# Row sums of relu: the last 16 rows of each partition in five pieces instead of seven

## The chip, the cores and the metric

The kernel runs on one core of one Trainium2 chip. The metric is the device time of one execution in microseconds (us), the median of several runs. A profile of one execution stands beside it: a record of what each engine and each DMA did, with its own span, which is shorter than the device time.

Engines that matter here: ScalarE (ACT in the profile), VectorE (DVE) and SyncE (SP), whose queue issues all the DMAs. TensorE does nothing. The 16 DMA engines move data between the chip's main memory (HBM) and the on-chip memory of 128 partitions (SBUF).

## The reference

```python
x = np.random.randn(32, 512, 1024).astype(np.float32)

def reference(x):
    relu_x = np.maximum(x, 0)
    return np.sum(relu_x, axis=-1).astype(np.float32)
```

There are 32 x 512 = 16384 rows of 1024 fp32 numbers, 67.1 MB. Each row gives one number, the sum of its positive elements. Every element is read once, so the work is a stream from HBM with a little arithmetic behind it.

## The kernel before

The 16384 rows are spread over 128 partitions, 128 rows each (`J`). They are taken in three regions (`REGIONS`): 1, 111 and 16 rows of each partition. Within a region, a partition's rows lie one after another in HBM, so a DMA of n rows has one contiguous run of n x 4096 bytes for each partition.

The first 112 rows of a partition come in seven chunks of 16 rows (`CHUNKS`, DMAs at L91) into three buffers of `buf` (`NB`), used in turn. SP waits on `s_dve` until a buffer has been read before it issues the DMA that overwrites it. Six chunks are worked on by both engines in series: ACT writes relu in place (L145), DVE sums it (L160). From chunk 6 on, each engine does whole rows by itself in one instruction with an accumulated sum: `on_act` (L127) is an activation with `accum_out`, `on_dve` (L130) a tensor_scalar with max and add. Each such instruction is followed by a short read of its accumulator, which appears as a line of its own in the profile.

The last region, 16 rows of each partition, is the tail. It goes into the buffer that chunk 4 had, and all its loads are issued one behind the other by SP when that buffer is free, at about 122 us; they queue behind chunk 6. There are seven pieces:

- 8, 4 and 2 rows (`TAIL`, L101). Each has its own semaphore. When a piece is in, DVE takes its even rows and ACT its odd rows (L184), each sum going straight into its column of `res`.
- The last two rows, 2048 columns of each partition, in four pieces. `first` is columns 0 to 912 (`CUT`), `second` is 1536 to 2048, `third` is 1280 to 1536, all into `buf` (L112). The fourth, columns 912 to 1280, goes into a small tensor `seam` (L115), from its third column on.

These two rows are cut in ways that do not follow the rows, so partial sums are needed. `first` is halved: ACT sums columns 0 to 456 into `seam` column 0, DVE 456 to 912 into `seam` column 1. ACT sums `second` and DVE sums `third` into the two last columns of `seam`. In `seam` the partial sums of the first row then stand to the left of that row's remaining 112 columns, and those of the second row to the right of its remaining 256 columns. One last instruction on each engine sums such a stretch (relu leaves the partial sums, which are not negative, as they are): ACT 2 + 112 = 114 columns for the first row, DVE 256 + 2 = 258 for the second. Both wait until `s_seam` is 16 + 2, which is the seam piece (16) and the two sums of `second` and `third`; ACT waits for `s_half` too, for the halves of `first`.

Results leave in three stores from `res`. The first 128 rows go early (through `turned`, L117). The 111 columns of the middle region are stored at L123 once chunk 6 is summed and the semaphore `s_in[-1]` says that `third` is in, so that the store is not ahead of the last loads. The last 16 columns are stored at L207 after both last instructions (`s_last`). SP then waits for all stores.

The order on each engine is the order in which the program is written. There is no scheduler.

Of the kernel before, what the change touches and what calls it, by code (L numbers as in the profile page):

```python
# [3 lines left out]
P = 128  # L4
D = 1024
BIG = 16
NB = 3
REGIONS = [1, 111, 16]
CHUNKS = [[(0, 0, 1), (1, 0, 15)]] + [[(1, 16 * c + 15, 16)] for c in range(6)]
ACT_STEPS = [[16], [7, 9], [7, 9], [7, 9], [4, 5, 7], [3, 4, 5]]  # L10
DVE_STEPS = [[4, 5, 7], [7, 4, 5], [7, 4, 5], [7, 4, 5], [4, 5, 7], [3, 4, 5]]
TAIL = [8, 4, 2]
CUT = 912
HEAD = 256


def bass_relu_sum_kernel(
# [14 lines left out]
    fp32 = mybir.dt.float32  # L32
# [4 lines left out]
    B, S, _ = x.shape  # L37
    J = B * S // P
    NBIG = len(CHUNKS)
    assert BIG * NBIG + sum(TAIL) + 2 == J == sum(REGIONS)  # L40

    xr = x.rearrange("b s d -> (b s) d")
    of = out.rearrange("b s -> (b s)")
# [1 line left out]
    xv = [  # L45
        xr[P * s : P * (s + n), :].rearrange("(p j) d -> p j d", p=P)
        for s, n in zip(start, REGIONS)
    ]
    ov = [of[P * s : P * (s + n)].rearrange("(p j) -> p j", p=P) for s, n in zip(start, REGIONS)]

    buf = nc.alloc_sbuf_tensor("buf", [P, NB, BIG, D], fp32)
    w = D - CUT
    seam = nc.alloc_sbuf_tensor("seam", [P, 2 + w + HEAD + 2], fp32)
    res = nc.alloc_sbuf_tensor("res", [P, J], fp32)
    turned = nc.alloc_sbuf_tensor("turned", [P, 32], fp32)

    n_in = NBIG + len(TAIL) + 3
    s_in = [nc.alloc_semaphore(f"s_in{i}") for i in range(n_in)]
    s_act = nc.alloc_semaphore("s_act")
    s_dve = nc.alloc_semaphore("s_dve")  # L60
    s_fact = nc.alloc_semaphore("s_fact")
    s_fdve = nc.alloc_semaphore("s_fdve")
    s_half = nc.alloc_semaphore("s_half")
    s_seam = nc.alloc_semaphore("s_seam")
    s_last = nc.alloc_semaphore("s_last")
    s_turn = nc.alloc_semaphore("s_turn")
# [3 lines left out]
    sp, act, dve = nc.sync, nc.scalar, nc.vector  # L70
# [5 lines left out]
    tb = NBIG % NB  # L76
# [8 lines left out]
    for c in range(NBIG + 1):  # L85
        if c >= NB:
            sp.wait_ge(s_dve, done[c - NB])
        if c < NBIG:
            i = 0
            for g, j, n in CHUNKS[c]:  # L90
                sp.dma_start(  # L91
                    out=buf[:, c % NB, i : i + n, :], in_=xv[g][:, j : j + n, :]
# [5 lines left out]
    r = 0  # L98
    tail = []
    for i, n in enumerate(TAIL):  # L100
        sp.dma_start(out=buf[:, tb, r : r + n, :], in_=xv[-1][:, r : r + n, :]).then_inc(  # L101
# [3 lines left out]
        r += n  # L105


    rows = xv[-1].rearrange("p j d -> p (j d)")[:, r * D : (r + 2) * D]
    flat = buf[:, tb, r : r + 2, :].rearrange("p j d -> p (j d)")
    first, second, third = [(0, CUT), (D + D // 2, 2 * D), (D + HEAD, D + D // 2)]  # L110
    for k, (lo, hi) in enumerate((first, second, third)):
        sp.dma_start(out=flat[:, lo:hi], in_=rows[:, lo:hi]).then_inc(  # L112
            s_in[NBIG + len(TAIL) + k], 16
        )
    sp.dma_start(out=seam[:, 2 : 2 + w + HEAD], in_=rows[:, CUT : D + HEAD]).then_inc(s_seam, 16)  # L115
    sp.wait_ge(s_turn, 1)
    sp.dma_start(  # L117
        out=of[0:P].rearrange("(k q) -> k q", q=32), in_=turned[0:P:32, 0:32]
# [7 lines left out]
    def on_act(t, acc):  # L126
        return act.activation(t, t, AF.Relu, accum_out=acc)  # L127

    def on_dve(t, acc):
        return dve.tensor_scalar(  # L130
            out=t, in0=t, scalar1=0.0, scalar2=None, op0=ALU.max, op1=ALU.add, accum_out=acc
        )
# [4 lines left out]
    k = 0  # L137
    for c in range(NTWO):
        alone = BIG - sum(ACT_STEPS[c])
        act.wait_ge(s_in[c], 16 * len(CHUNKS[c]))  # L140
        r = 0
        ready = []
        for n in ACT_STEPS[c]:
            t = buf[:, c % NB, r : r + n, :]
# [10 lines left out]
        r = seen = 0  # L155
        for n in DVE_STEPS[c]:
            if ready[r + n - 1] > seen:
# [3 lines left out]
                out=res[:, c * BIG + r : c * BIG + r + n],  # L161
                in_=buf[:, c % NB, r : r + n, :],
# [17 lines left out]
    for r, n, s in tail:  # L180
        act.wait_ge(s, 16)
        dve.wait_ge(s, 16)
        for i in range(r, r + n):
            f = on_act if (i - r) % 2 else on_dve  # L184
            f(buf[:, tb, i, :], res[:, j0 + i : j0 + i + 1])

    lo, hi = first
    act.wait_ge(s_in[-3], 16)
    dve.wait_ge(s_in[-3], 16)
    on_act(flat[:, lo : CUT // 2], seam[:, 0:1]).then_inc(s_half, 1)  # L190
    on_dve(flat[:, CUT // 2 : hi], seam[:, 1:2]).then_inc(s_half, 1)
    k = 2 + w
    lo, hi = second
    act.wait_ge(s_in[-2], 16)
    on_act(flat[:, lo:hi], seam[:, k + HEAD : k + HEAD + 1]).then_inc(s_seam, 1)
    lo, hi = third
    dve.wait_ge(s_in[-1], 16)
    on_dve(flat[:, lo:hi], seam[:, k + HEAD + 1 : k + HEAD + 2]).then_inc(s_seam, 1)
    act.wait_ge(s_seam, 16 + 2)
    act.wait_ge(s_half, 2)  # L200
    on_act(seam[:, 0:k], res[:, J - 2 : J - 1]).then_inc(s_last, 1)
    dve.wait_ge(s_seam, 16 + 2)
    on_dve(seam[:, k : k + HEAD + 2], res[:, J - 1 : J]).then_inc(s_last, 1)


    sp.wait_ge(s_last, 2)
# [31 lines left out]
```

## Time and profile before

| | |
|---|---|
| median of 3 runs | 160.8 us (160.77 to 160.82) |
| span of the profiled execution | 159.4 us |
| read from HBM | 67.11 MB, 421 GB/s over the span |
| DVE busy | 120.6 us (76%) |
| ACT busy | 101.5 us (64%) |

The span is 1.4 us shorter than the median time. The page's issue list gives for each load the time from its issue by SP to its landing; sizes are those of all partitions together, so 456.0 KB are 912 columns of 128 partitions:

```profile
buf<-in_x_dram SPq DMA_DIRECT2D x1, 4096.0 KB, 25.3
buf<-in_x_dram SPq DMA_DIRECT2D x1, 2048.0 KB, 29.9
buf<-in_x_dram SPq DMA_DIRECT2D x1, 1024.0 KB, 31.9
buf<-in_x_dram SPq DMA_DIRECT2D x1, 456.0 KB, 32.5
buf<-in_x_dram SPq DMA_DIRECT2D x1, 256.0 KB, 32.7
seam<-in_x_dram SPq DMA_DIRECT2D x1, 184.0 KB, 32.6
```

They are long because the loads wait in the queue behind chunk 6, 8 MB that are still coming in. A line of the profile's list of instructions gives the start, the duration, the engine, the source line, the operation, the tile written and the tile read, and the shape; in brackets stands how long the engine was idle before it and what ended that.

### The profile page before, as it was taken

The page shows a single profiled execution, that of the slowest core. Times are in us where ns is not written, and L with a number is a line of the kernel's source. Part 1 is how long each engine was busy: PE and PEld are TensorE (multiplying, and loading weights), DVE is VectorE, ACT ScalarE, POOL GpSimd, SP SyncE. Part 2 cuts the span into 40 slices and gives each one's busy share as a digit, 9 for nine tenths or more (in the row PEclk, how much of TensorE's full clock was granted, in tenths as well). Part 3 has the DMA queues.
Part 4 walks back from the last instruction along what each step waited for, and adds up shares of the span by engine and source line. Part 5 has one row for each costly group of instructions (what it writes and reads, how often), then busy time and mean ns, then how long its engine had stood idle before and what let it go on. Part 6 is the DMA issues. An engine that isn't in the chain of part 4 may idle for free.

```text
span 159.4 us, 150 instructions
## 1 busy us (share of the span) xinstructions
DVE 120.6 (76%) x59; ACT 101.5 (64%) x54; POOL 0.2 (0%) x4
## 2 busy tenths in 40 slices
DVE  0000000009999999999999999999999999898995
ACT  3000059980799708996099941999329980496975
POOL 0000000000000000000000000000000000000000
DMA  9997996996996997989979969969969979798994
GB/s 378 493 401 339 493 526 263 526 526 263 526 493 296 526 444 345 526 378 411 526 312 477 526 263 526 526 263 526 526 263 526 444 345 526 321 469 374 417 400 142
DMA packets 2457, 67.18 MB, mean 421 GB/s; under 512 B 536, under 2 KB 792, under 8 KB 1176
## 3 DMA queue, kind: packets, MB, share of 16 engines
q1 hardware_dynamic: 2456, 67.18, 98.1%
q14 instruction: 1, 0.01, 0.0%
HBM read 67.11 MB, written 0.07 MB: 421 GB/s over the span
## 4 chain that ended last, share of the span: by engine, by line
DVE 55%; DMA 34%; ACT 9%; SPq 2%; issue 0%
DVE res L160 54%; DMA buf<-in_x_dram 34%; ACT buf L145 9%; SPq L101 1%; SPq L112 1%; DVE buf L130 0%; DVE seam L130 0%; SPq L91 0%; DVE turned L169 0%
## 5 line engine op out<-in xcount | busy, mean ns | idle before, releaser
L160 DVE TENSOR_REDUCE res<-buf 128x4 f32<-128x4096 f32 (+3 forms) x18 | 99.4, 5596 | 35.5 <-ACT buf L145 35.5
L145 ACT ACTIVATE buf<-buf 128x7168 f32<-128x7168 f32 (+5 forms) x13 | 80.4, 6233 | 46.1 <-DMA buf<-in_x_dram 46.1
L127 ACT ACTIVATE buf<-buf 128x1024 f32<-128x1024 f32 (+2 forms) x19 | 19.0, 999 | 8.9 <-DMA buf<-in_x_dram 8.9
L130 DVE TENSOR_SCALAR_CACHE_REDUCE buf<-buf 128x1024 f32<-128x1024 f32 (+2 forms) x19 | 20.7, 1143 | 1.7 <-DMA buf<-in_x_dram 1.6
L127 ACT ACTIVATION_READ_ACCUMULATOR buf<-buf 128x1 f32 x19 | 3.6, 188 | 0.0
L145 ACT ACT_TABLE_LOAD x1 | 1.3, 1283 | 1.3 <-PEq L223 1.3
L130 DVE DVE_READ_ACCUMULATOR buf<-buf 128x1 f32 x19 | 1.6, 84 | 0.0
L130 DVE TENSOR_SCALAR_CACHE_REDUCE seam<-seam 128x258 f32<-128x258 f32 x1 | 0.4, 421 | 0.0
L127 ACT ACTIVATE seam<-seam 128x114 f32<-128x114 f32 x1 | 0.3, 300 | 0.1
L169 DVE STREAM_TRANSPOSE turned<-res 128x32 f32<-128x32 f32 x1 | 0.2, 211 | 0.0
L127 ACT ACTIVATION_READ_ACCUMULATOR seam<-seam 128x1 f32 x1 | 0.2, 186 | 0.0
L223 POOL MEMSET const-bfloat16-1.0<- 128x1 bf16 x1 | 0.1, 101 | 0.0
L223 POOL MEMSET const-uint8-127<- 128x1 uint8 x1 | 0.1, 101 | 0.0
L223 POOL MEMSET const-float32-0.0<- 128x1 f32 x1 | 0.1, 98 | 0.2 <-issue 0.2
L223 POOL MEMSET const-float32-1.0<- 128x1 f32 x1 | 0.1, 98 | 0.0
L130 DVE DVE_READ_ACCUMULATOR seam<-seam 128x1 f32 x1 | 0.1, 82 | 0.0
## 6 DMA issues: line engine op xcount, KB each, us to landing
buf<-in_x_dram SPq DMA_DIRECT2D x1, 7680.0 KB, 21.1
buf<-in_x_dram SPq DMA_DIRECT2D x1, 4096.0 KB, 25.3
buf<-in_x_dram SPq DMA_DIRECT2D x1, 2048.0 KB, 29.9
buf<-in_x_dram SPq DMA_DIRECT2D x1, 1024.0 KB, 31.9
buf<-in_x_dram SPq DMA_DIRECT2D x1, 512.0 KB, 3.3
buf<-in_x_dram SPq DMA_DIRECT2D x1, 456.0 KB, 32.5
buf<-in_x_dram SPq DMA_DIRECT2D x1, 256.0 KB, 32.7
seam<-in_x_dram SPq DMA_DIRECT2D x1, 184.0 KB, 32.6
```

Of the source, the lines that this page charges most:

```text
L101: sp.dma_start(out=buf[:, tb, r : r + n, :], in_=xv[-1][:, r : r + n, :]).then_inc(s_in[NBIG + i], 16)
L112: sp.dma_start(out=flat[:, lo:hi], in_=rows[:, lo:hi]).then_inc(s_in[NBIG + len(TAIL) + k], 16)
L127: return act.activation(t, t, AF.Relu, accum_out=acc)
L130: return dve.tensor_scalar(out=t, in0=t, scalar1=0.0, scalar2=None, op0=ALU.max, op1=ALU.add, accum_out=acc)
L145: act.activation(t, t, AF.Relu).then_inc(s_act, 1)
L160: dve.tensor_reduce(out=res[:, c * BIG + r : c * BIG + r + n], in_=buf[:, c % NB, r : r + n, :], axis=X, op=ALU.add,).then_inc(s_dve, 1)
L169: dve.transpose(out=turned[:, :], in_=res[:, 0:32]).then_inc(s_turn, 1)
L223: nc = _bacc.Bacc("TRN2", target_bir_lowering=False, num_devices=1)
```

## The change

The three whole-row pieces of the tail become two, and the last two rows in four pieces become the last three rows in three pieces:

- 9 and 4 rows (`TAIL`), where the pieces were 8, 4 and 2. The roles in a piece are swapped: ACT takes the even rows, DVE the odd ones.
- Of the last three rows, 3072 columns: columns 0 to 1884, then 2304 to 3072 (768 columns) into `buf`, and last columns 1884 to 2304 (420 columns) into `seam` (`ENDS`), from its second column on.

When the 1884 columns are in, DVE sums the first of the three rows whole, and ACT sums the second row's 860 columns into `seam` column 0. When the 768 columns of the third row are in, ACT sums 432 of them (`SPLIT`) and DVE 336, into the two last columns of `seam`. The last pair is then 1 + 164 = 165 columns on ACT and 256 + 2 = 258 on DVE. It waits for the seam piece and the three partial sums (`s_seam`, 16 + 3). `s_half` is gone. The store of 111 columns now waits for the 768 columns, which `s_in[-1]` now stands for.

```diff
-TAIL = [8, 4, 2]
-CUT = 912
-HEAD = 256
+TAIL = [9, 4]
+ENDS = [1884, 2304]
+SPLIT = 432
...
-    w = D - CUT
-    seam = nc.alloc_sbuf_tensor("seam", [P, 2 + w + HEAD + 2], fp32)
+    lo, hi = ENDS
+    w = hi - lo
+    seam = nc.alloc_sbuf_tensor("seam", [P, 1 + w + 2], fp32)
...
-    rows = xv[-1].rearrange("p j d -> p (j d)")[:, r * D : (r + 2) * D]
-    flat = buf[:, tb, r : r + 2, :].rearrange("p j d -> p (j d)")
-    first, second, third = [(0, CUT), (D + D // 2, 2 * D), (D + HEAD, D + D // 2)]
-    for k, (lo, hi) in enumerate((first, second, third)):
-        sp.dma_start(out=flat[:, lo:hi], in_=rows[:, lo:hi]).then_inc(
+    rows = xv[-1].rearrange("p j d -> p (j d)")[:, r * D : (r + 3) * D]
+    flat = buf[:, tb, r : r + 3, :].rearrange("p j d -> p (j d)")
+    for k, (f, t) in enumerate(((0, lo), (hi, 3 * D))):
+        sp.dma_start(out=flat[:, f:t], in_=rows[:, f:t]).then_inc(
             s_in[NBIG + len(TAIL) + k], 16
         )
-    sp.dma_start(out=seam[:, 2 : 2 + w + HEAD], in_=rows[:, CUT : D + HEAD]).then_inc(s_seam, 16)
+    sp.dma_start(out=seam[:, 1 : 1 + w], in_=rows[:, lo:hi]).then_inc(s_seam, 16)
...
-            f = on_act if (i - r) % 2 else on_dve
+            f = on_dve if (i - r) % 2 else on_act
             f(buf[:, tb, i, :], res[:, j0 + i : j0 + i + 1])
 
-    lo, hi = first
-    act.wait_ge(s_in[-3], 16)
-    dve.wait_ge(s_in[-3], 16)
-    on_act(flat[:, lo : CUT // 2], seam[:, 0:1]).then_inc(s_half, 1)
-    on_dve(flat[:, CUT // 2 : hi], seam[:, 1:2]).then_inc(s_half, 1)
-    k = 2 + w
-    lo, hi = second
     act.wait_ge(s_in[-2], 16)
-    on_act(flat[:, lo:hi], seam[:, k + HEAD : k + HEAD + 1]).then_inc(s_seam, 1)
-    lo, hi = third
+    dve.wait_ge(s_in[-2], 16)
+    on_dve(flat[:, 0:D], res[:, J - 3 : J - 2])
+    on_act(flat[:, D:lo], seam[:, 0:1]).then_inc(s_seam, 1)
+
+    act.wait_ge(s_in[-1], 16)
     dve.wait_ge(s_in[-1], 16)
-    on_dve(flat[:, lo:hi], seam[:, k + HEAD + 1 : k + HEAD + 2]).then_inc(s_seam, 1)
-    act.wait_ge(s_seam, 16 + 2)
-    act.wait_ge(s_half, 2)
-    on_act(seam[:, 0:k], res[:, J - 2 : J - 1]).then_inc(s_last, 1)
-    dve.wait_ge(s_seam, 16 + 2)
-    on_dve(seam[:, k : k + HEAD + 2], res[:, J - 1 : J]).then_inc(s_last, 1)
+    on_act(flat[:, hi : hi + SPLIT], seam[:, 1 + w : 2 + w]).then_inc(s_seam, 1)
+    on_dve(flat[:, hi + SPLIT : 3 * D], seam[:, 2 + w : 3 + w]).then_inc(s_seam, 1)
+
+    cut = 1 + 2 * D - lo
+    act.wait_ge(s_seam, 16 + 3)
+    on_act(seam[:, 0:cut], res[:, J - 2 : J - 1]).then_inc(s_last, 1)
+    dve.wait_ge(s_seam, 16 + 3)
+    on_dve(seam[:, cut : 3 + w], res[:, J - 1 : J]).then_inc(s_last, 1)
```

More of the change, by code (lines that the diff above doesn't have):

```diff
@@ L39, in bass_relu_sum_kernel @@
     NBIG = len(CHUNKS)
-    assert BIG * NBIG + sum(TAIL) + 2 == J == sum(REGIONS)
+    assert BIG * NBIG + sum(TAIL) + 3 == J == sum(REGIONS)
     xr = x.rearrange("b s d -> (b s) d")
@@ L51, in bass_relu_sum_kernel @@
     buf = nc.alloc_sbuf_tensor("buf", [P, NB, BIG, D], fp32)
-    w = D - CUT
-    seam = nc.alloc_sbuf_tensor("seam", [P, 2 + w + HEAD + 2], fp32)
+    lo, hi = ENDS
+    w = hi - lo
+    seam = nc.alloc_sbuf_tensor("seam", [P, 1 + w + 2], fp32)
     res = nc.alloc_sbuf_tensor("res", [P, J], fp32)
     turned = nc.alloc_sbuf_tensor("turned", [P, 32], fp32)
-    n_in = NBIG + len(TAIL) + 3
+    n_in = NBIG + len(TAIL) + 2
     s_in = [nc.alloc_semaphore(f"s_in{i}") for i in range(n_in)]
@@ L62, in bass_relu_sum_kernel @@
     s_fdve = nc.alloc_semaphore("s_fdve")
-    s_half = nc.alloc_semaphore("s_half")
     s_seam = nc.alloc_semaphore("s_seam")
```

## The prediction, made before the changed kernel was run

> **What bounds the kernel now.** I read four views in this order: the page's row of busy tenths with the table of DMA queues, the chain that ended last, the timeline of the last 12 us, and the groups kept apart by shape for the prices.
>
> ```profile
> DMA  9997996996996997989979969969969979798994
> q1 hardware_dynamic: 2456, 67.18, 98.1%
> ```
>
> The DMA engines are busy over the whole span, so the input stream sets when the last rows arrive. What the engines do after that is all that this change can move.
>
> ```profile
> 123.39 0.44 SPq L112
> ...
> 123.88 0.46 SPq L112
> ...
> 124.39 32.60 DMA buf<-in_x_dram
> 156.99 0.02 issue
> 157.01 0.44 DVE buf L130 x2
> 157.45 0.02 issue
> 157.47 0.43 DVE seam L130 x2
> ```
>
> This is the end of the chain of waits (start us, us, what). The last piece of `buf` lands at 156.99, DVE works on it until 157.45, and the seam instruction closes the sum. The issue steps show that an engine starts 0.02 us after the landing that it waits for; I fold this into each landing below, so "in at 147.43" means that a waiting engine starts then.
>
> ```profile
> 137.72 1.06 ACT L127 ACTIVATE buf<-buf 128x1024 f32<-128x1024 f32 x1 [6.65 <-DMA buf<-in_x_dram]
> ...
> 147.43 1.06 ACT L127 ACTIVATE buf<-buf 128x1024 f32<-128x1024 f32 x1 [1.29 <-DMA buf<-in_x_dram]
> 147.43 1.22 DVE L130 TENSOR_SCALAR_CACHE_REDUCE buf<-buf 128x1024 f32<-128x1024 f32 x1 [0.51 <-DMA buf<-in_x_dram]
> 148.40 0.19 ACT L127 ACTIVATION_READ_ACCUMULATOR buf<-buf 128x1 f32 x1
> 148.49 1.04 ACT L127 ACTIVATE buf<-buf 128x1024 f32<-128x1024 f32 x1
> ...
> 152.32 1.06 ACT L127 ACTIVATE buf<-buf 128x1024 f32<-128x1024 f32 x1 [0.62 <-DMA buf<-in_x_dram]
> ...
> 154.84 1.06 ACT L127 ACTIVATE buf<-buf 128x1024 f32<-128x1024 f32 x1 [0.32 <-DMA buf<-in_x_dram]
> ...
> 155.96 0.58 ACT L127 ACTIVATE buf<-buf 128x456 f32<-128x456 f32 x1
> 155.98 0.08 DVE L130 DVE_READ_ACCUMULATOR buf<-buf 128x1 f32 x1
> 155.98 0.62 DVE L130 TENSOR_SCALAR_CACHE_REDUCE buf<-buf 128x456 f32<-128x456 f32 x1
> 156.45 0.19 ACT L127 ACTIVATION_READ_ACCUMULATOR buf<-buf 128x1 f32 x1
> 156.53 0.08 DVE L130 DVE_READ_ACCUMULATOR buf<-buf 128x1 f32 x1
> 156.65 0.63 ACT L127 ACTIVATE buf<-buf 128x512 f32<-128x512 f32 x1
> 157.01 0.42 DVE L130 TENSOR_SCALAR_CACHE_REDUCE buf<-buf 128x256 f32<-128x256 f32 x1 [0.40 <-DMA buf<-in_x_dram]
> ```
>
> The brackets give the idle time before an instruction and its releaser. Both engines wait at every piece of the tail: 8 rows in at 147.43, 4 at 152.32, 2 at 154.84, the 912 columns at 155.96, the 512 at 156.65, the 256 at 157.01. The seam piece is issued at 124.87 and takes 32.6 us to land, so it is in at about 157.47, level with DVE, whose accumulator read ends at 157.44.
>
> **The pace of the stream.** From 137.72 (chunk 6 in) to 147.43 is 9.71 us for 8 rows, 1.214 us a row; then 4.89 us for 4 rows, 1.22 a row; 2.52 us for 2 rows, 1.23 ns a column. The small pieces come at 1.12 us for 912 columns (1.23 ns), 0.69 for 512 (1.35), 0.36 for 256 (1.41) and 0.46 for the seam's 368 (1.25).
>
> **Step 1, the first piece has 9 rows.** In at 137.72 + 9 x 1.214 = 148.65, 1.22 us later than now. ACT now takes rows 0, 2, 4, 6, 8: five rows, where it had four. The first row after a wait costs it 1.06 us, each further one 1.04 (starts 147.43, 148.49, 149.53). It is free at 148.65 + 1.06 + 4 x 1.04 = 153.87. DVE has four rows, 1.15 and then 1.14 each (147.43, 148.58, 149.72), free at 153.22.
>
> [...]
>
> **Step 2, four rows.** In at 148.65 + 4.89 = 153.54, before ACT is free (153.87) but after DVE is (153.22). ACT runs two rows until 153.87 + 2 x 1.04 = 155.95; DVE waits 0.32 us and runs until 153.54 + 1.15 + 1.14 = 155.83.
>
> **Step 3, 1884 columns.** At 1.23 ns a column 2.32 us, in at 155.86 (at the seam's 1.25 it is 155.90). DVE takes a whole row from 155.86 and can start its next at 157.01. ACT takes 860 columns. Its shapes of 1024 and 456 columns took 1041 and 584 ns, those of 512 and 114 took 630 and 300: 0.80 to 0.83 ns a column, so the step is 1.04 - 164 x 0.82 ns = 0.91 us, until 156.86.
>
> **Step 4, 768 columns.** Between the 912 and 512 rows, 1.12 and 0.69 us, a line gives 0.97 us; in at 156.83 (1.23 ns gives 156.80, 1.35 gives 156.90). ACT, free at 156.86, runs 432 columns: the 456 ran from 155.96 to the end of its accumulator read at 156.64, 0.68 us; 24 columns less make 0.66, done at 157.52. DVE runs 336 columns: the 256 took 157.01 to 157.44, 0.43; the 456 took 155.98 to 156.61, 0.63; between them 0.51, done at 157.52.
>
> **Step 5, the seam piece of 420 columns.** At 1.23 to 1.41 ns 0.52 to 0.59 us, in at 157.35 to 157.42. It is hidden behind both engines by 0.10 us or more; without that cover each later tenth would count in full.
>
> **Step 6, the last pair.** It starts 0.03 us after the later engine, at 157.55, where it was 157.47. DVE's instruction keeps its 258 columns and its 0.43 us; ACT's grows from 114 to 165 columns, 0.04 us, from 0.40 (157.47 to 157.87) to 0.44. Done at 157.99, against 157.90 (DVE's read ends 157.82 + 0.08). The store issue and its 1.4 us to landing are unchanged.
>
> **Edits at no cost.** Two issues fewer on SP (0.44 us each) lie at 122 to 126 us, while chunk 6 is still streaming until 137.7; without that cover they would be 0.9 us. The store of 111 columns now waits for the 768 piece instead of the 256 and is issued some 0.15 us sooner. Its semaphore is not what SP waits for last (SP's last wait is 1.1 us on the last store), so nothing is gained there; if it met the seam piece in the DMA engines it would use up the 0.10 us of cover. `s_half` goes away with its wait on ACT, which was met at 156.61 (end of DVE's 456 columns), long before 157.47.
>
> **Sum.** Gate +0.08, last pair +0.01, together +0.09 us: span 159.4 + 0.09 = 159.5, and with the 1.4 us between the span and the median of 160.8, 160.89. Two prices are not in the trace. A wait on ACT that is already met when ACT comes to it: for DVE at 155.98 it cost nothing (1.14 us after 154.84, its ordinary step); ACT's start at 155.96 stands 0.07 after the 155.89 of its own pace, which the landing explains. So 0 to 0.07 at each of three such waits, 0 to 0.21; I take 0, as DVE shows. Second, the landings: rounding of the pace over 9 rows is -0.04 (1.21) to +0.08 (1.222) on everything behind it, and the 768 piece at its slow bound adds 0.04.
>
> [...]
>
> **Rivals.** A, ACT has no slack any more (slower). In this forecast ACT never waits from 148.65 on: 7 rows, 860, 432. For it speaks that margins at the last two landings are 0.09 and 0.03 us; against it, that DVE's met wait cost nothing. With 0.07 at each of three met waits, and the 768 piece 0.04 late, ACT ends 0.25 later: 161.14. It passes 0.2% (0.32 us, about what a measurement of this kernel tells from no change) from 0.08 us per wait alone.
>
> B, the stream alone sets the end (faster). Five pieces instead of seven could let all 16 rows come at 1.214 us: 137.72 + 19.42 = 157.14, 0.33 before the present 157.47, 160.48. For it: the last 2048 columns now take 2.63 us where two rows at 1.214 take 2.43. Against it: ACT's seven rows and two pieces after 148.65 do not get shorter, so the gain would have to reach the 9-row landing too.
>
> C, the engines sit where I put them but the seam piece is late, for it lands at an odd offset (one column into the seam, not two). At 1.41 ns it is hidden; it would have to land at twice the 0.46 us of the present one, 0.92, to set the gate at 157.75 and give 161.1, so it decides only beyond that.
>
> **How the numbers follow.** The forecast, 160.89 with 160.80 to 161.05 of its own, has a chance of 0.64; A 0.20, C 0.06, B 0.10. Slower by over 0.2% is most of A (0.17), half of C (0.03) and 0.02 for the forecast's own unknowns, 0.22; faster is B where its pieces gain slightly more than the rows show (0.08); 0.70 is left for within 0.2%. The range reaches from 160.68, part of the way to B, to 161.15, which holds most of A.
>
> **What would show it.** Step 1: both engines start at 148.65, ACT's next wait is for the seam. Step 2: DVE idle 0.3 us before 153.54, ACT none. Steps 3 and 4: 860 starts at 155.95 and 432 at 156.86 on ACT; 336 at 157.01 on DVE. Step 6: the last pair at 157.55. The forecast is wrong if ACT shows gaps above 0.05 us between 148.65 and 157.5, if the 9 rows land off 148.65 by 0.15 us, or if the seam's instructions wait for their piece.

## The result, and the profile after

The changed kernel takes 161.20 us, the median of 16 runs (161.00 to 161.46), against 160.85 us of the kernel before, run beside it. The ratio is 1.0019, 95% interval 1.0012 to 1.0025. So it is slower, by about 0.2%, and clear of no change. The forecast was 160.89, with a range up to 161.15: wrong by 0.31 us, where the forecast change was 0.09.

The first question is whether the tail went as forecast. The end of the chain of waits of the changed kernel (start us, us, what):

```profile
122.55 31.07 DMA buf<-in_x_dram
153.61 0.02 issue
153.64 3.96 DVE buf L129 x8
157.59 0.02 issue
157.62 0.43 ACT seam L126 x2
```

From 153.64 on the chain is engine work without a wait: eight DVE records (four instructions and their accumulator reads), then the last pair. Before, the chain went through the stream until 156.99. The timeline of the changed kernel shows the same step by step:

```profile
148.75 1.06 ACT L126 ACTIVATE buf<-buf 128x1024 f32<-128x1024 f32 x1 [2.50 <-DMA buf<-in_x_dram]
...
152.92 1.04 ACT L126 ACTIVATE buf<-buf 128x1024 f32<-128x1024 f32 x1
...
153.64 1.22 DVE L129 TENSOR_SCALAR_CACHE_REDUCE buf<-buf 128x1024 f32<-128x1024 f32 x1 [0.24 <-DMA buf<-in_x_dram]
...
153.96 1.04 ACT L126 ACTIVATE buf<-buf 128x1024 f32<-128x1024 f32 x1
...
155.00 1.04 ACT L126 ACTIVATE buf<-buf 128x1024 f32<-128x1024 f32 x1
...
156.03 0.90 ACT L126 ACTIVATE buf<-buf 128x860 f32<-128x860 f32 x1
...
156.94 0.55 ACT L126 ACTIVATE buf<-buf 128x432 f32<-128x432 f32 x1
...
157.08 0.50 DVE L129 TENSOR_SCALAR_CACHE_REDUCE buf<-buf 128x336 f32<-128x336 f32 x1
...
157.62 0.34 ACT L126 ACTIVATE seam<-seam 128x165 f32<-128x165 f32 x1
157.62 0.42 DVE L129 TENSOR_SCALAR_CACHE_REDUCE seam<-seam 128x258 f32<-128x258 f32 x1
...
158.08 0.34 SPq L204 DMA_DIRECT2D out_dram<-res  x1
```

ACT has no idle time in brackets after 148.75. Everything lies 0.07 to 0.10 us behind the forecast, evenly, because the 9 rows were in at 148.75 instead of 148.65 in this execution. The last store is issued at 158.08, against 157.93 before, 0.15 us later, and the span is 159.5 against 159.4.

That is less than half of the 0.35 us between the medians. The rest is not in the span. Each run lists its time beside its span: the median time is 161.2 us and the median span 159.5, so 1.6 to 1.7 us lie around the span, where the prediction had carried over 1.4. (The spans are listed to 0.1 us.) The page has one more difference, easily passed over, in its table of DMA queues. Before:

```profile
q14 instruction: 1, 0.01, 0.0%
HBM read 67.11 MB, written 0.07 MB: 421 GB/s over the span
```

After:

```profile
q1 hardware_dynamic: 2168, 67.18, 97.9%
HBM read 67.11 MB, written 0.07 MB: 421 GB/s over the span
```

Within the span of the kernel before, one packet (8 KB) came over a queue named "instruction", called the packet of instructions below after that name; what it holds is not in the profile. In the span of the changed kernel there is none; in its trace such a packet starts at 160.9, behind the span. In the trace of the kernel before it starts at 159.2, just ahead of the span's end.

### The profile page after: what moved, and what is told of

It reads as the page before. It is cut to its first block, busy times and chain, and to the rows that moved or that the text cites. A ratio compares the mean times of both kernels' runs of the same rounds, so it can differ in the third digit from the quotient of the medians.

```text
span 159.5 us, 145 instructions
## 1 busy us (share of the span) xinstructions
DVE 120.0 (75%) x57; ACT 101.4 (64%) x54; POOL 0.2 (0%) x4
## 4 chain that ended last, share of the span: by engine, by line
DVE 57%; DMA 33%; ACT 9%; SPq 0%; issue 0%
DVE res L159 54%; DMA buf<-in_x_dram 33%; ACT buf L144 9%; DVE buf L129 2%; ACT seam L126 0%; SPq L91 0%; SPq L101 0%; DVE turned L168 0%
## 5 line engine op out<-in xcount | busy, mean ns | idle before, releaser
L129 DVE TENSOR_SCALAR_CACHE_REDUCE buf<-buf 128x1024 f32<-128x1024 f32 (+1 forms) x18 | 20.1, 1177 | 2.4 <-DMA buf<-in_x_dram 2.4
## 6 DMA issues: line engine op xcount, KB each, us to landing
seam<-in_x_dram SPq DMA_DIRECT2D x1, 210.0 KB, 33.4
```

Of the source, the lines that this page charges most:

```text
L129: return dve.tensor_scalar(out=t, in0=t, scalar1=0.0, scalar2=None, op0=ALU.max, op1=ALU.add, accum_out=acc)
```

## The experiments

The changed kernel differs from the one before in the number of its instructions too. DVE has one summing instruction less, and with its accumulator read two less (the pages count 59 and 57). ACT has one less, the separate wait that `s_half` needed (57 and 56 in the traces, waits counted). SP has two DMAs less (22 and 20). Below, a "met" wait is one whose condition already holds when the engine comes to it, so that it adds an instruction and no waiting. The theories: the loss is in the tail (tail theory), or around the span and tied to some engine's number of instructions (outside theory). "Outside" below is a run's time less its span.

**Both kernels again, on one chip.**

> The kernel before, unchanged, so that its time and span stand beside those of the changed kernel from one chip. Tail theory (the 0.35 us are lost inside the span, in the last 12 us): span 159.4, time 160.85, 1.4 us outside the span. Outside theory (about half of the 0.35 lies behind the last instruction of the kernel, in the engines' closing sequence): the same here. Start theory (the 0.1 us by which the changed kernel's first chunk landed later is chance): the first chunk's landing varies by 0.1 us between this profile and the first one, 21.59.

> The changed kernel, unchanged. Tail theory: spans are 0.3 us longer than those of the kernel before, 159.7, and the rest outside is 1.4 us. Outside theory: spans are 0.05 to 0.15 longer, and what lies outside the span is 1.6 to 1.7 us, 0.2 more. Start theory: the first chunk lands at 21.6 in some profiles, and then the span is 159.43.

**The changed kernel, counts of ACT and SP restored.**

```diff
+    for i in range(1, 5):
+        sp.wait_ge(s_in[i], 16)
     sp.wait_ge(s_turn, 1)
...
     j0 = NBIG * BIG
+    act.wait_ge(s_in[1], 16)
```

> The changed kernel with waits added that are long met, so that ACT and SP again have as many instructions as before (one more, two more). Nothing in the tail changes. Outside theory, if ACT's or SP's count of instructions sets the closing sequence: 1.4 us outside the span again, time 161.0. Tail theory, or if it is DVE's count: as the changed kernel, 161.2.

**The changed kernel, count of DVE restored.**

```diff
+    pad = nc.alloc_sbuf_tensor("pad", [P, 8], fp32)
...
+    for i in range(2):
+        dve.memset(pad[:, i : i + 1], 0.0)
     k = 0
     for c in range(NTWO):
```

> The changed kernel with two memsets of one column added on DVE ahead of its first work, where it idles for 35 us, so that DVE again has as many instructions as before. Nothing in the tail changes. Outside theory, if DVE's count of instructions sets the closing sequence: 1.4 us outside the span again, time 161.0. Tail theory, or if it is ACT's or SP's count: as the changed kernel, 161.2.

What these four gave, with the count of each engine against the kernel before:

| kernel | ACT, DVE, SP | median us | mean span | outside, mean (range) |
|---|---|---|---|---|
| before, 33 runs beside them | 0, 0, 0 | 160.84 | 159.49 | 1.36 (1.32 to 1.41) |
| before again | 0, 0, 0 | 160.82 | 159.49 | 1.35 (1.31 to 1.42) |
| changed again | -1, -2, -2 | 161.08 | 159.55 | 1.60 (1.48 to 1.78) |
| ACT and SP restored | 0, -2, 0 | 161.07 | 159.50 | 1.57 (1.41 to 1.71) |
| DVE restored | -1, 0, -2 | 161.03 | 159.53 | 1.50 (1.47 to 1.55) |

The tail theory falls: the mean spans differ by 0.05 us, the means outside by 0.24. The start theory holds in part: of the two profiles of the changed kernel as it stands, one has the first chunk in at 21.70 and the 9 rows at 148.75, the other 21.59 and 148.65. Here is the second, the end of its chain of waits, from a page whose span is 159.4 us like that of the kernel before:

```profile
122.08 26.55 DMA buf<-in_x_dram
148.63 0.02 issue
148.65 8.84 ACT buf L126 x18
157.49 0.02 issue
157.51 0.43 ACT seam L126 x2
```

This is the forecast's chain: in at 148.65, ACT's nine instructions (18 records with the accumulator reads) without a gap, the last pair at 157.51, where 157.55 was forecast.

The outside theory was not borne out as I had put it, one engine's count being the cause. Restoring DVE took away the spread and 0.10 of the mean; restoring ACT and SP alone took away 0.03. The queue table of the kernel with DVE restored has its line back, and the one with ACT and SP restored has not:

```profile
q1 hardware_dynamic: 2168, 67.18, 97.9%
q14 instruction: 1, 0.01, 0.0%
```

So in these four the time of this packet goes with DVE's count. The runs that follow agree: in the traces the packet starts at 159.2 to 159.4 in all ten profiles with DVE's count as before or one more, at 160.8 to 160.9 in all four with one or two less (the one with one less has a second packet at 161.2), and at 143.1 in both with eight more.

**Both restored, and ACT and SP apart.**

> The changed kernel with both additions: two memsets ahead of DVE's work, one met wait more on ACT and two on SP. Outside theory, now with two parts (a part that varies, up to 0.25 us, goes with DVE's count; a fixed 0.14 goes with ACT's or SP's): both gone, 1.36 us outside the span in every run, median 160.85 to 160.92. Tail theory: the 0.2 to 0.3 stay, 161.05 to 161.2.

> The changed kernel with DVE's two memsets and ACT's one wait, SP as changed. If the fixed 0.14 goes with ACT's count: 1.36 us outside, median 160.9. If with SP's: 1.50 outside, median 161.03.

> The changed kernel with DVE's two memsets and SP's two instructions, ACT as changed. If the fixed 0.14 goes with SP's count: 1.36 us outside, median 160.9. If with ACT's: 1.50 outside, median 161.03.

**The kernel before with one instruction less on ACT.**

```diff
-    on_act(flat[:, lo : CUT // 2], seam[:, 0:1]).then_inc(s_half, 1)
-    on_dve(flat[:, CUT // 2 : hi], seam[:, 1:2]).then_inc(s_half, 1)
+    on_act(flat[:, lo : CUT // 2], seam[:, 0:1]).then_inc(s_seam, 1)
+    on_dve(flat[:, CUT // 2 : hi], seam[:, 1:2]).then_inc(s_seam, 1)
...
-    act.wait_ge(s_seam, 16 + 2)
-    act.wait_ge(s_half, 2)
+    act.wait_ge(s_seam, 16 + 4)
...
-    dve.wait_ge(s_seam, 16 + 2)
+    dve.wait_ge(s_seam, 16 + 4)
```

> The kernel before, with the two halves of the first piece counted on s_seam instead of s_half (both last instructions wait for 16 + 4), so that ACT has one instruction less and nothing in the tail moves. If the fixed 0.14 goes with ACT's count: 1.50 us outside the span and a median of 160.97, from this alone. If with SP's or DVE's: 1.36 and 160.83.

| kernel | ACT, DVE, SP | median us | ratio to before (95%) | mean span | outside, mean (range) |
|---|---|---|---|---|---|
| before, 33 runs beside them | 0, 0, 0 | 160.81 | | 159.45 | 1.36 (1.31 to 1.41) |
| changed, all restored | 0, 0, 0 | 160.86 | 1.0007 (0.9998 to 1.0016) | 159.53 | 1.38 (1.33 to 1.42) |
| changed, DVE and ACT restored | 0, 0, -2 | 160.91 | 1.0007 (0.9999 to 1.0016) | 159.55 | 1.37 (1.33 to 1.41) |
| changed, DVE and SP restored | -1, 0, 0 | 161.03 | 1.0014 (1.0005 to 1.0023) | 159.53 | 1.52 (1.46 to 1.56) |
| before, ACT one less | -1, 0, 0 | 160.94 | 1.0011 (1.0002 to 1.0020) | 159.47 | 1.52 (1.50 to 1.54) |

With DVE and ACT restored the changed kernel comes out where the prediction had it: 160.86 and 160.91, 0.05 and 0.10 us above the kernel before, and 1.37 or 1.38 us outside. SP's two DMAs do not matter to this. The last row is the cross-check: the kernel before, its tail and all its arithmetic left alone, loses 0.13 us in the median by one wait less on ACT; the mean span grows by 0.02 and the mean outside by 0.16. This edit also drops the semaphore `s_half` itself. That is not the cause: the changed kernel has dropped it too, and with the counts of DVE and ACT restored it has 1.37.

**Is a shorter program bad, or any other?**

> The changed kernel with one met wait more on ACT and one memset on DVE: ACT as many instructions as before, DVE one less than before (the changed kernel has two less, the accumulator reads counted). Threshold theory (the closing sequence is late when an engine's program falls short of some length): 1.36 us outside the span if the length needed is reached with one, else 1.45 with a spread of 0.2. Exact theory (only the very count of before is good): above 1.36 with a spread.

> The kernel before with one met wait more on ACT. Threshold theory: longer does no harm, 1.36 us outside the span, median 160.83. Exact theory: as with one less, 1.5 outside, 160.95.

> The kernel before with one memset more on DVE, ahead of its work. Threshold theory: 1.36 us outside the span, median 160.83. Exact theory: 1.45 or more, with a spread of 0.2.

> The kernel before with eight memsets more on DVE and three instructions more on ACT, all in their idle time. Threshold theory: 1.36 us outside the span still, median 160.83 (a lower value would mean that padding alone makes a faster kernel). Exact theory: 1.5 or more.

Then, since one of these had the packet of instructions in the middle of the stream, its two additions apart (the same loops of memsets and of met waits as above, with eight memsets, and with six waits, which make three instructions):

> The kernel before with the eight memsets on DVE alone. If DVE's longer program makes its load of instructions fall into the stream: the 8-row piece is in 0.6 us late, as with both additions (10.35 us after chunk 6 instead of 9.7), span 160.0, time 161.4. If it is ACT's: span 159.4 and 1.36 us outside, 160.83.

> The kernel before with three instructions more on ACT alone. If ACT's longer program makes its load of instructions fall into the stream: span 160.0 and the 8-row piece 0.6 us late. If that was DVE's: span 159.4, and outside the span 1.36 if ACT's closing is in time, up to 1.9 if it is late as in half of the runs with one instruction more.

| kernel | ACT, DVE, SP | median us | mean span | outside, mean (range) |
|---|---|---|---|---|
| changed, ACT restored, DVE one of two | 0, -1, -2 | 161.41 | 159.54 | 1.84 (1.65 to 1.97) |
| before, ACT one more | +1, 0, 0 | 160.90 | 159.45 | 1.60 (seven runs 1.36 to 1.45, five 1.80 to 1.96) |
| before, ACT three more | +3, 0, 0 | 160.97 | 159.49 | 1.49 (1.40 to 1.60) |
| before, DVE one more | 0, +1, 0 | 160.81 | 159.46 | 1.38 (1.33 to 1.41) |
| before, DVE eight more | 0, +8, 0 | 161.43 | 160.08 | 1.36 (1.33 to 1.40) |
| before, both | +3, +8, 0 | 161.54 | 160.06 | 1.49 (1.39 to 1.58) |

The kernel before, beside them, had 160.83 and 160.82, with 1.36 and 1.37 outside. The rows with 161.41, 161.43 and 161.54 rest on five runs each.

Neither the threshold nor the exact theory holds for both engines. For DVE a longer program does no harm outside the span (1.38 us with one more, 1.36 with eight), and a shorter one does, one less (1.84) more than two (1.57). For ACT every other count that I tried was worse, one less (1.52), one more (1.60) and three more (1.49). With one more the runs fell into two groups, which neither theory had; with three more they have 1.49, neither the 1.36 nor the 1.9 that was expected. Padding alone made nothing faster, and no version was found that beats the kernel before.

The kernel with eight memsets shows what else the count moves. Its timeline has

```profile
137.79 1.06 ACT L128 ACTIVATE buf<-buf 128x1024 f32<-128x1024 f32 x1 [6.67 <-DMA buf<-in_x_dram]
...
148.10 1.06 ACT L128 ACTIVATE buf<-buf 128x1024 f32<-128x1024 f32 x1 [1.89 <-DMA buf<-in_x_dram]
```

The 8-row piece is in 148.10 - 137.79 = 10.31 us after chunk 6, where the kernel before has 9.71 (147.43 - 137.72): 0.60 us late, and everything behind it too. The queue table of its window from 137 to 149 says what is different:

```profile
q1 hardware_dynamic: 214, 5.10, 98.8%
q14 instruction: 1, 0.01, 0.2%
```

The same window of the kernel before has only

```profile
q1 hardware_dynamic: 216, 5.13, 99.2%
```

The packet of instructions, which had come at 159.2, now comes within the stream (in the trace it starts at 143.07 and lasts 0.31 us). The trace also shows a packet that is delayed. The 8-row piece is 128 packets of 32 KB; 127 of them took 1.21 or 1.22 us, and the one that starts at 143.38, where the packet of instructions ends, took 1.80. The kernel with both additions has the same pair (143.11, then a packet of 1.78 us at 143.42). The kernel before has none over 1.22.

The kernel with three instructions more on ACT alone has this packet at 159.3 and its mean span at 159.49: it is DVE's count that moves this one. But it has a second packet, at 160.7, behind the span. Its queue table from 159 to 161 has

```profile
q14 instruction: 2, 0.02, 2.6%
```

The kernel with both additions has a second one too, at 161.3, and the one with eight memsets alone has not. So in these two a further packet goes with ACT's three.

## Why the prediction was wrong, point by point

**Steps 1 to 4, right.** The two profiles of the changed kernel have the 9 rows in at 148.65 and 148.75 (forecast 148.65), ACT without a gap from there, 860 columns from 155.94 and 156.03 (155.95), 432 from 156.84 and 156.94 (156.86), 336 on DVE from 156.97 and 157.08 (157.01). DVE's idle time ahead of the four rows was 0.24 us in the first profile (0.32).

**Step 5, right.** Nothing waited for the seam piece in either chain: in the first profile it was in at about 157.4 (issued at 124.01, 33.4 us to landing), and both engines ended at 157.58.

**Step 6 and the sum in the span, right in sign, somewhat too large.** The last pair started at 157.51 and 157.62 (157.55). On one chip the mean span grew by 0.05 us (159.49 to 159.55) where 0.09 was forecast. One reading of the prediction was too broad, though no number rests on it: "Both engines wait at every piece of the tail". Its own lines show that DVE came to the 912 columns at its ordinary pace (155.98), and that only ACT took the 512 and only DVE the 256.

**"Edits at no cost", wrong.** The step said that `s_half` goes away with its wait on ACT, at no cost since the wait was long met, and it priced DVE's missing instruction only by the work that it does. Neither takes time on the path inside the span. But they change how many instructions the two programs have, and that moved what happens behind the span. One less on ACT costs 0.16 us outside by itself (1.36 to 1.52 in the kernel before, its tail and its other counts as they were); with DVE's count right and ACT's wrong the changed kernel has 1.50 and 1.52. Two less on DVE cost 0.19 (1.38 to 1.57, ACT and SP being restored), and bring the spread between runs, which the kernel before does not have. The two do not add up: with both the changed kernel has 1.60, 0.24 more than before. SP's two DMAs less were free as forecast (1.37 against 1.38).

**"With the 1.4 us between the span and the median", wrong, and this is the term of the sum that failed.** It was carried over as a constant, without a reason. It is 1.36 in the kernel before and 1.60 to 1.64 in the changed one. The sum with the measured values is 160.85 + 0.05 (span) + 0.24 (outside) = 161.14, against 161.08 and 161.20 as medians of the two sets of runs.

**Rival A** would also have ended at 161.14, but for another reason, and the traces refute it: ACT's starts at 152.92, 153.96, 155.00 and 156.03 are 1.04 us apart across two met waits. **Rival B** fell with ACT's chain, as argued against it. **Rival C** fell with step 5. Two transfers fewer brought no gain: the mean span was 159.55 us, against 159.49.

The traces show updates of semaphores behind the span. Those of semaphores 156 to 206 begin 0.31 us after the end of the span in the kernel before and in the changed kernel with DVE restored, and 0.72 to 0.73 in the changed kernel and in that with ACT and SP restored. They follow DVE's count, as the packet of instructions does. In the two kernels with three instructions more on ACT it is the updates of semaphores 54 to 104 that are late, at 0.78 instead of 0.34 or 0.35. What these updates are for is not in the traces.

For one instruction less on ACT the traces show where the time goes. Semaphore 2 is updated fourteen times behind the span. In every profile whose ACT count is not one less, the last but one of these updates comes 0.03 us after the one before it. In all five with one less it comes 0.16 to 0.18 us after. In the kernel before, the last update thereby moves from 1.46 us behind the span to 1.59, which is 0.13 of the 0.16. The loss that goes with two less on DVE is not in these updates: with ACT and SP restored the last one comes at 1.46, as before, in a run with 1.70 outside. Just ahead of the span, from 0.38 us before its start, the updates of semaphore 2 are the same to 0.01 us in all kernels.

**What stays open.** Why DVE's count moves the updates of semaphores 156 to 206 and costs time is not shown. These late updates do not wait for the packet of instructions to arrive: in the changed kernel they are over at 1.02 us behind the span, and the packet starts at 1.39. For ACT, why one less delays that one step, and why one more gives two groups, is open; the packet goes with three more, but no packet was seen that goes with one less. All the padding stood ahead of the tail, so the runs do not tell the number of instructions from the place in the program at which the last ones stand. Chunk 6 was in at 137.72 in some profiles and up to 0.18 us later in others, of the changed kernel's variants and of some of the kernel before; this was not traced further.

## What to carry to other kernels

The span is not the whole time. Here the rest lay between 1.35 and 1.84 us on average, a difference of 0.3% of the kernel. For changes of that size take each run's time less its span as a second measurement, and look there first when a change whose trace agrees with the forecast is still slower. An edit that takes an instruction away is not free by that alone (one wait less on ACT cost 0.13 us of the median here, 160.94 against 160.81); before a tail is reworked for a tenth of a microsecond, pad both versions to the same number of instructions on each engine, in idle time, and compare those. Such a padded pair also tells what the edit itself is worth (here 0.05 to 0.10 us lost, in intervals that just take in no loss at all). The padding has to be measured too: one wait more on ACT in the kernel before, and eight memsets more on DVE, made it slower (160.90 against 160.83, and 161.43 against 160.82).

## What the runs showed of the hardware

A single 8 KB packet of the queue "instruction" that fell into the input stream (whose packets took 98.8% of the DMA engines' time from 137 to 149 us) made an 8-row piece 0.60 us late, twice what the packet itself took (0.31 us): the 32 KB packet behind it took 1.80 us instead of 1.21. The whole kernel was 0.6 us slower (161.43 against 160.82, ratio 1.0039, 1.0027 to 1.0052). Eight small memsets in 35 us of idle time on DVE were enough to bring it there.

One more met wait on ACT, placed at a point where ACT idles (6.65 us ahead of chunk 6 in the kernel before), gave two groups of runs of the same program, 0.45 us apart outside the span (seven at 1.36 to 1.45, five at 1.80 to 1.96), with equal spans (159.4 to 159.5). A met wait on an engine that is busy cost nothing inside the span: ACT's starts across two of them stayed 1.04 us apart, and DVE passed one, in the kernel before, 1.14 us after its last start (154.84 to 155.98), its ordinary step.
